# Scores of two query tiles in one three-bank PSUM tile, and two banks for projections, in the attention of a two-layer first block

## The chip, the cores and the metric

The kernel runs on one core of one Trainium2 chip. The metric is the device time of one execution in microseconds. One core has five engines that work side by side, each through its own queue in order: TensorE (PE, matmuls; its weight loads are shown apart as PEld), VectorE (DVE), ScalarE (ACT), GpSimd (POOL) and SyncE (SP, which issues most of the DMAs). Matmul results land in PSUM, which is 8 banks of 512 fp32 columns on 128 partitions; all eight are allotted in this kernel.

## The reference, cut to what matters

Two blocks follow each other on 512 tokens of width 1024: a first block of two layers, and a second block with one attention layer and a mixture of 32 experts. The change touches the first block alone. Each of its layers does this (x is 512 tokens, xc a context of 256 tokens; the second layer needs no output for the context):

```
h  = rms_norm(x)  * (1 + scale)   + shift        # scale, shift, gate: silu(c) @ w_mod + b_mod
hc = rms_norm(xc) * (1 + scale_c) + shift_c
parts = split(h @ w_in)                          # q and kv latents, gates, two convolution branches
k, v  = context and x tokens concatenated        # 256 + 512 = 768 keys, 8 heads of 96 (values of 64)

s = einsum('bqhd,bkhd->bhqk', q, k) * 96 ** -0.5
p = softmax(s, axis=-1)
attn = einsum('bhqk,bkhd->bqhd', p, v)

y = concat([attn * silu(g_a), short_conv_branch, long_conv_branch])
x = x + gate * (y @ w_out)                       # layer 0 does the same for xc, with the 256 context keys
```

## The kernel before

**Precision.** Every large product is made of three matmuls (`mm3`, lines 220 to 222): operands are split into a high and a low part (`split`: ACT writes the high part on line 183, DVE the low part on line 184), and high*high, high*low and low*high are added up in PSUM.

**A layer** (`layer`) first makes queries, keys and values and stores them in DRAM, while the projections `cf_a`, `cf_g` and `g_a` run beside that. Then comes the stretch that the change touches, the attention. It is a loop over 8 heads and, within a head, over groups of two query tiles of 128 tokens: three groups in layer 0 (two on the 512 x tokens with 768 keys, and g == 2 on the 256 context tokens with 256 keys), two groups in layer 1. That makes 24 steps in layer 0 and 16 in layer 1.

**One step.** `mla_scores` makes the scores `pS` of both query tiles (6 matmuls each for 768 keys: a piece of 512 columns and one of 256), DVE takes the negated row maximum (line 917) and scales it (918), ACT takes the exponential from PSUM into `P` with its row sum (920), DVE inverts the sum (921) and POOL scales `P` (922). `mla_out` then transposes `P` on PE, four 128x128 blocks to a bank (`pPT`, line 935), splits each bank into `PTh` (ACT) and `PTl` (DVE), and multiplies by the values (`pO`, line 945). The loop issues the scores of step s + 1 ahead of the transposes of step s. Between these pieces it lets other work in (`late`, a `Fill`, which hands out pieces by their cost): the remaining ten column projections (`cm`, bank `pcm`) and matmuls on the modulation weights (`mod_part`, bank `pmod`, read by ACT into `mrow` on line 329). At the end of the loop `norm_conv` (`pmean`, `pvar`, `prs`, `ppw`) finishes the long convolution branch. After the layer come `mod_gate` (`pgate`, line 355) and the output projection `out_proj` (`pout`).

**Order.** Nobody writes the order of these instructions down. The program gives them in the order of the code, and a scheduler with a cost model sorts them for each engine; the engines then run their queues strictly in order. A tile from a pool waits until the readers of the tile that had its place are done, and an instruction that writes a part of a tile waits for earlier readers of that tile.

**PSUM before.** Tag A: two tiles of two banks (`pa`: each query tile's scores has one, of which 768 of 1024 columns are used; also `pmean`, `prs`, `pkv`, `pq`, `pout`). Tag T: two banks (`pt`: transposes). Tag C: one bank (`pc`: `pcm`, `pmod`, `ppw`). Tag O: one bank (`po`: `pO`).

Of the kernel before, what the change touches and what calls it, by code (L numbers as in the profile page):

```python
# [10 lines left out]
F32 = mybir.dt.float32  # L11
# [20 lines left out]
PS2 = (3, 2, 2)  # L32
# [28 lines left out]
class Fill:  # L61
# [3 lines left out]
    def __init__(self, gens):  # L65
        self.gens, self.ready, self.debt = list(gens), [], 0.0
# [45 lines left out]
class K:  # L112
    def __init__(self, tc, I, out):
        self.tc, self.nc, self.I, self.out = tc, tc.nc, I, out
        self.es = ExitStack()
        self.nlo = 0
        self.single = False

    def pool(self, name, side=None, space=None, reuse="tile"):
        kw = {}  # L120
# [8 lines left out]
    def setup(self):  # L129
# [11 lines left out]
        self.ones = cp.tile([128, 128], F32, name="ones")  # L141
        nc.vector.memset(self.ones, 1.0 / 256)

    def pa(self, name="pa"):
        return self.ps.tile([128, 1024], F32, name=name, tag="A", bufs=2)

    def second_banks(self):
# [15 lines left out]
        return self.ps.tile([128, 512], F32, name=name, tag="T", bufs=PS2[1] if self.single else 2)  # L163

    def pc(self, name="pc"):
        return self.ps.tile([128, 512], F32, name=name, tag="C", bufs=PS2[2] if self.single else 1)

    def po(self, name="po"):
        return self.ps.tile([128, 512], F32, name=name, tag="O", bufs=1)
# [299 lines left out]
    def layer(self, l, hT, wl):  # L469
# [25 lines left out]
        for nm in ("q_head_norm_w", "k_head_norm_w"):  # L495
            w = self.brow(tr, I[nm][l][64:96], 32, "w32" + nm[0])
            t = tr.tile([128, 4, 2, 32], F32, name="tab" + nm[0])
# [11 lines left out]
        segs = [(0, 512)] if last else [(0, 512), (512, 256)]  # L509
# [183 lines left out]


        ap = self.pool(f"attn{l}", side="right")
        if not last:
            self.tables(ap)
        projs = [f(i) for i in range(2) for f in (sc_in, sc_c, sc_b, g_b)]
# [75 lines left out]

        for _ in tail:
            pass
        ap.release()
        lp.release()
        gp.release()
# [122 lines left out]
    def mla_scores(self, qkv, g, ap):  # L902

        nc, sp = self.nc, self.sp
        Q, Kt = qkv["q"], qkv["k"]
        segs = ((512, 768),) if g == 2 else ((0, 512), (512, 768))
        Ps = []
        for t in (2 * g, 2 * g + 1):
            pS = self.pa("pS")
            k0 = segs[0][0]  # L910
            for c0, c1 in segs:
                self.mm3(pS[:, c0 - k0:c1 - k0], [x[:, t * 128:(t + 1) * 128] for x in Q], [x[:, c0:c1] for x in Kt],
                         True, True)
            S = pS[:, :768 - k0]
            P = ap.tile([128, 768], F32, name="P", tag="P", bufs=PB)[:, :768 - k0]
            nm = sp.tile([128, 1], F32, name="nm", bufs=4)
            nc.vector.tensor_reduce(nm, S, axis=AX.X, op=OP.max, negate=True)  # L917
            nc.vector.tensor_scalar(nm, nm, SM1, None, op0=OP.mult)  # L918
            l = sp.tile([128, 1], F32, name="ll", bufs=4)
            nc.scalar.activation(P, S, AF.Exp, bias=nm, scale=SM1, accum_out=l)  # L920
            nc.vector.reciprocal(l, l)  # L921
            nc.gpsimd.tensor_scalar(P, P, l, 0.5, op0=OP.mult, op1=OP.mult)  # L922
            Ps.append(P)
        return Ps
# [1249 lines left out]
```

## Time and profile before

| | us |
|---|---|
| median of 3 runs | 1450.34 (1446.74 to 1450.8) |
| the profiled execution, whole | 1445.97 |
| its span, from the first to the last instruction | 1444.2 |
| attention of layer 0, first scores to last (start of the first matmul to the start of the last) | 181.5 to 416.3 |
| attention of layer 1, the same | 620.1 to 759.9 |

The profiled execution lies 4.4 us under the median and within the range of the runs; 1.8 us of it lie outside the span. A row of the timeline gives the start, the duration, the engine, the line of the kernel, the operation, what it writes and reads, how many were merged, and in square brackets how long the engine had been idle and what released it. Matmuls are pipelined: the time from one start to the next is what a matmul takes of PE, and the duration in the row is longer.

### The profile page before, as it was taken

What the parts mean: (1) busy time and instruction counts of PE and PEld (TensorE: products, weight loads), DVE (VectorE), ACT (ScalarE), POOL (GpSimd) and SP (SyncE); (2) the same over time, 40 slices, a digit from 0 to 9 for tenths busy, and PEclk for the clock granted to TensorE, in tenths of its full rate; (3) what the DMA queues carried; (4) which work ended last, traced back from release to release, by engine and by line L of the source; (5) the groups of instructions that cost most, each with busy time, mean ns of one, the idle gap of its engine ahead of it and who ended that gap; (6) DMA issues with size and microseconds to landing.
All of it is one profiled execution on the core that took longest, in us unless ns stands there. A gap on an engine that the chain in (4) does not pass through costs nothing. (4 is left out here: it accounts for less than half of the span.)

```text
span 1444.2 us, 22627 instructions
## 1 busy us (share of the span) xinstructions
PE 1313.0 (91%) x8030; PEld 1039.8 (72%) x8030; DVE 963.3 (67%) x2272; ACT 614.8 (43%) x1198; POOL 311.3 (22%) x397
## 2 busy tenths in 40 slices
PE   4999999998979999899999999999997999999873
PEld 2888777876867788677877788887777877675441
DVE  4689997565652589998775645777677553454555
ACT  4554255544641375256574335776654111112112
POOL 2332032222230134123322111111111111111101
PEclk9999999998999999999999999999998999999987
DMA  8643345435231255416144365323545689999971
GB/s 291 201 128 114 99 133 158 122 102 147 77 140 42 93 127 153 147 45 163 39 131 149 124 200 133 81 81 124 183 157 195 224 292 373 375 368 389 390 279 59
DMA packets 166917, 246.46 MB, mean 171 GB/s; under 512 B 46774, under 2 KB 102918, under 8 KB 166804
## 3 DMA queue, kind: packets, MB, share of 16 engines
q1 hardware_dynamic: 161460, 235.07, 49.3%
q0 software_dynamic: 4768, 7.84, 1.9%
q10 hardware_dynamic: 576, 2.10, 0.4%
q8 instruction: 64, 1.05, 0.3%
q14 instruction: 49, 0.40, 0.1%
HBM read 221.74 MB, written 33.33 MB: 177 GB/s over the span
## 5 line engine op out<-in xcount | busy, mean ns | idle before, releaser
L184 DVE TENSOR_TENSOR wlo<-wraw,whi 128x1024 fp32r<-128x1024 f32 (+3 forms) x98 | 119.0, 1220 | 60.6 <-ACT whi L183 60.1
L183 ACT ACTIVATE whi<-wraw 128x1024 fp32r<-128x1024 f32 (+3 forms) x98 | 100.6, 1036 | 106.2 <-PE pout L222 42.6
L922 POOL TENSOR_SCALAR P<-P,ll 128x768 f32<-128x768 f32 (+1 forms) x80 | 76.3, 958 | 187.0 <-DVE ll L921 103.3
L220 PE MATMUL pcm<-hTh,whi 128*128 128x256 f32 (+1 forms) x288 | 103.6, 360 | 9.9 <-DVE oa L529 4.3
L569 DVE SCALAR_TENSOR_TENSOR za<-zp,vec,za 128x783 f32<-128x783 f32 (+1 forms) x120 | 109.1, 916 | 0.5
L222 PE MATMUL pcm<-hTh,wlo 128*128 128x256 f32 (+1 forms) x288 | 100.1, 347 | 0.2 <-DVE wlo L184 0.2
L221 PE MATMUL pcm<-hTl,whi 128*128 128x256 f32 (+1 forms) x288 | 99.4, 345 | 0.0
L184 DVE TENSOR_TENSOR PTl<-pPT,PTh 128x512 fp32r<-128x512 f32 x104 | 70.3, 683 | 24.0 <-ACT PTh L183 23.7
L183 ACT ACTIVATE PTh<-pPT 128x512 fp32r<-128x512 f32 x104 | 60.2, 595 | 53.9 <-PE pPT L935 48.3
L920 ACT ACTIVATE P<-pS,nm 128x768 f32<-128x768 f32 (+1 forms) x80 | 64.9, 814 | 35.9 <-DVE nm L918 30.9
L1815 POOL DMA_INDIRECT xg<-h2d,tok x32 | 31.6, 987 | 207.8 <-PE pturn L1799 119.2
L917 DVE TENSOR_REDUCE nm<-pS 128x1 f32<-128x768 f32 (+1 forms) x80 | 66.4, 844 | 14.9 <-PE pS L222 14.2
L1421 POOL TENSOR_SCALAR P<-P,l 128x384 f32<-128x384 f32 (+1 forms) x64 | 34.2, 547 | 182.2 <-DVE m L1417 116.7
L220 PEld LDWEIGHTS pcm<-hTh,whi 128*128 128x128 f32 x288 | 55.5, 193 | 17.4 <-DVE oa L529 4.9
L220 PE MATMUL pcm<-hT0h,whi 128*128 128x512 f32 x144 | 59.3, 412 | 7.9 <-DVE oa L529 5.8
L935 PE MATMUL pPT<-ident,P 128*128 128x128 f32 x416 | 63.5, 279 | 3.3 <-POOL P L922 2.5
L1832 PE MATMUL pgu<-exT,eraw 128*128 128x128 f32 x512 | 60.9, 279 | 0.0
L222 PEld LDWEIGHTS pcm<-hTh,wlo 128*128 128x128 f32 x288 | 55.6, 193 | 6.8 <-DVE wlo L184 0.6
L1832 PEld LDWEIGHTS pgu<-exT,eraw 128*128 128x128 f32 x512 | 59.3, 194 | 1.3 <-DVE exT L1810 0.6
L221 PEld LDWEIGHTS pcm<-hTl,whi 128*128 128x128 f32 x288 | 55.5, 193 | 4.9 <-issue 0.2
L222 PE MATMUL pcm<-hT0h,wlo 128*128 128x512 f32 x144 | 58.0, 403 | 0.0
L221 PE MATMUL pcm<-hT0l,whi 128*128 128x512 f32 x144 | 57.9, 402 | 0.0
(535 smaller groups left out, 3670.7 us busy)
## 6 DMA issues: line engine op xcount, KB each, us to landing
wraw<-in_w_in_dram SPq DMA_DIRECT2D x56, 512.0 KB
eraw<-in_w_expert_gate_dram SPq DMA_DIRECT2D x52, 512.0 KB
eraw<-in_w_expert_up_dram SPq DMA_DIRECT2D x52, 512.0 KB
wraw<-in_w_mod_dram SPq DMA_DIRECT2D x48, 512.0 KB
wl<-in_w_expert_down_dram SPq DMA_DIRECT2D x32, 512.0 KB
wh<-in_w_expert_down_dram SPq DMA_DIRECT2D x32, 512.0 KB
wraw<-in_w_out_dram SPq DMA_DIRECT2D x24, 512.0 KB
wraw<-in_w_expert_gate_dram SPq DMA_DIRECT2D x12, 512.0 KB
```

What stands on the lines that cost most here:

```text
L183: nc.scalar.activation(hi, src, AF.Copy)
L184: return (eng or nc.vector).tensor_tensor(lo, src, hi.bitcast(F32), op=OP.subtract)
L220: mm(out, lhs[0], rhs[0], start=start, stop=False)
L221: mm(out, lhs[0], rhs[1], start=False, stop=False)
L222: mm(out, lhs[1], rhs[0], start=False, stop=stop)
L569: nc.vector.scalar_tensor_tensor(a[:, :nz], z[:, k:k + nz], cfw[:, i, k:k + 1], a[:, :nz], op0=OP.mult, op1=OP.add)
L917: nc.vector.tensor_reduce(nm, S, axis=AX.X, op=OP.max, negate=True)
L920: nc.scalar.activation(P, S, AF.Exp, bias=nm, scale=SM1, accum_out=l)
L922: nc.gpsimd.tensor_scalar(P, P, l, 0.5, op0=OP.mult, op1=OP.mult)
L935: nc.tensor.transpose(p[:, jj, i * 128:(i + 1) * 128], Ps[i][:, (j + jj) * 128:(j + jj + 1) * 128], self.ident)
L1421: nc.gpsimd.tensor_scalar(Ps[i], Ps[i], l[:, i:i + 1], 1.0, op0=OP.mult, op1=OP.mult)
L1832: self.last = self.nc.tensor.matmul(p[:, s, c, :], gu[2 * s + k // 4][:, k % 4, c * 128:(c + 1) * 128], x[:, k, :], start=(k == 0), stop=( ...
```

## The change

During the attention of both layers (from the point at which the projections ahead of it are done, to the end of `layer`) the PSUM pool is released and a pool with another division takes its place; at the end it is swapped back. In the new pool the scores have one tile of three banks (tag S, one buffer), the tag C has two banks, T two and O one. `mla_scores` now takes one tile for a step and puts the second query tile's scores behind the first's, at column 768, which is the middle of the second bank. Its pieces are cut at the bank's border: 256 and 512 columns in place of 512 and 256. The users of `pa` other than the scores (`pf` in `tables`, `pmean`, `prs`) take the tile S too while the attention runs.

```diff
+    def attention_banks(self, on):
+
+        self.ps.release()
+        self.ps = self.pool("psuma" if on else "psum", space=bass.MemoryType.PSUM)
+        self.attn = on
+
     def pa(self, name="pa"):
+        if self.attn:
+            return self.ps.tile([128, 1536], F32, name=name, tag="S", bufs=1)
         return self.ps.tile([128, 1024], F32, name=name, tag="A", bufs=2)
...
     def pc(self, name="pc"):
-        return self.ps.tile([128, 512], F32, name=name, tag="C", bufs=PS2[2] if self.single else 1)
+        return self.ps.tile([128, 512], F32, name=name, tag="C", bufs=2 if self.attn else PS2[2] if self.single else 1)
...
         ap = self.pool(f"attn{l}", side="right")
+        self.attention_banks(True)
...
         for _ in tail:
             pass
+        self.attention_banks(False)
         ap.release()
...
-        segs = ((512, 768),) if g == 2 else ((0, 512), (512, 768))
+        k0 = 512 if g == 2 else 0
         Ps = []
-        for t in (2 * g, 2 * g + 1):
-            pS = self.pa("pS")
-            k0 = segs[0][0]
-            for c0, c1 in segs:
+        pS2 = self.pa("pS")
+        for i, t in enumerate((2 * g, 2 * g + 1)):
+
+            pS = pS2[:, i * 768:i * 768 + 768]
+            for c0, c1 in ((512, 768),) if g == 2 else ((0, 256), (256, 768)) if i else ((0, 512), (512, 768)):
                 self.mm3(pS[:, c0 - k0:c1 - k0], [x[:, t * 128:(t + 1) * 128] for x in Q], [x[:, c0:c1] for x in Kt],
                          True, True)
```

The diff does not show what the scheduler makes of it. The number of matmuls, of reads of PSUM and of DMAs stays the same; their order moves on every engine. In the rows below a row is an instruction with its line, its output and inputs (the number behind a name is that of one tile), its size, and the semaphores on which it waits (`Activation` is ACT, `Pool` is POOL); "x4" is four alike.

PE, the last wide score pair of layer 0's head 7, before. Two tiles (4258 and 4273), their 12 matmuls back to back; the second tile waits only for the tile that had its place:

```order
L221 MATMUL pS_4258<-klo_3908,qhi_3911 128x512
L222 MATMUL pS_4258<-khi_3907,qlo_3912 128x512
L220 MATMUL pS_4258<-khi_3907,qhi_3911 128x256
L221 MATMUL pS_4258<-klo_3908,qhi_3911 128x256
L222 MATMUL pS_4258<-khi_3907,qlo_3912 128x256
L220 MATMUL pS_4273<-khi_3907,qhi_3911 128x512 [waits PE_49,Activation_49]
L221 MATMUL pS_4273<-klo_3908,qhi_3911 128x512
L222 MATMUL pS_4273<-khi_3907,qlo_3912 128x512
```

The same place now; both halves are the one tile 4240, and P_4170 and P_4184 are the two halves of the step before:

```order
L229 MATMUL pS_4240<-klo_3893,qhi_3896 128x512
L230 MATMUL pS_4240<-khi_3892,qlo_3897 128x512
L228 MATMUL pS_4240<-khi_3892,qhi_3896 128x256
L229 MATMUL pS_4240<-klo_3893,qhi_3896 128x256
L230 MATMUL pS_4240<-khi_3892,qlo_3897 128x256
L946 MATMUL pPT_4270<-ident_69,P_4184 128x128 [waits Pool_49]
L946 MATMUL pPT_4270<-ident_69,P_4170 128x128
L946 MATMUL pPT_4270<-ident_69,P_4184 128x128
L946 MATMUL pPT_4279<-ident_69,P_4184 128x128
L946 MATMUL pPT_4279<-ident_69,P_4170 128x128
L946 MATMUL pPT_4279<-ident_69,P_4184 128x128
L228 MATMUL pS_4240<-khi_3892,qhi_3896 128x256 [waits Activation_49]
```

The second half no longer follows the first: six transposes stand between them, and its first matmul waits for ACT.

PE, early in layer 0, where a modulation bank has been filled and read out (`mrow`) and a projection follows, before. There is one C bank, and `pcm_2293` needs it:

```order
L945 MATMUL pO_2166<-PTl_2212,vhl_1802 128x256 [waits DVE_49]
L945 MATMUL pO_2166<-PTl_2212,vhl_1802 128x256
L892 MATMUL pkT_2263<-ident_69,kraw_2123 96x128 [waits PE_49]
L892 MATMUL pkT_2263<-ident_69,kraw_2123 96x128
L222 MATMUL pS_2314<-khi_1794,qlo_1799 128x256
L220 MATMUL pcm_2293<-hTh_85,whi_2269 128x512 [waits PE_49,Activation_49]
L221 MATMUL pcm_2293<-hTl_86,whi_2269 128x512
L222 MATMUL pcm_2293<-hTh_85,wlo_2270 128x512 [waits DVE_49]
```

The first projection behind such a modulation bank now:

```order
L228 MATMUL pcm_2589<-hTh_85,whi_2552 128x512 [waits DVE_49,Activation_49]
L229 MATMUL pcm_2589<-hTl_86,whi_2552 128x512
L956 MATMUL pO_2165<-PTh_2171,vhl_1805 128x256 [waits DVE_49,Activation_49]
L956 MATMUL pO_2165<-PTh_2171,vhl_1805 128x256
L228 MATMUL pcm_2684<-hTh_85,whi_2552 128x256 [waits PE_49]
L229 MATMUL pcm_2684<-hTl_86,whi_2552 128x256
L230 MATMUL pcm_2589<-hTh_85,wlo_2553 128x512 [waits DVE_49]
L228 MATMUL pcm_2589<-hTh_85,whi_2552 128x512
```

Two projection tiles, 2589 and 2684, are open at once, in the two C banks.

PE at the end of layer 0's attention, before (`pout` is the output projection, `ppw` the last product of the long convolution branch):

```order
L222 MATMUL pS_4389<-khi_3907,qlo_3912 128x256
L220 MATMUL pout_4565<-whi_4490,hTh_85 128x512 [waits Activation_49]
L221 MATMUL pout_4565<-wlo_4491,hTh_85 128x512
L222 MATMUL pout_4565<-whi_4490,hTl_86 128x512
L220 MATMUL pout_4565<-whi_4490,hTh_85 128x512
L673 MATMUL ppw_4445<-lnd_4172,wraw_4357 128x512 [waits DMAHW1_49,DVE_49]
L935 MATMUL pPT_4461<-ident_69,P_4381 128x128 [waits Pool_49]
L221 MATMUL pout_4565<-wlo_4491,hTh_85 128x512
L222 MATMUL pout_4565<-whi_4490,hTl_86 128x512
L673 MATMUL ppw_4445<-lnd_4176,wraw_4357 128x512 [waits DVE_49]
```

And now, up to the first matmul of the output projection:

```order
L681 MATMUL ppw_4462<-lnd_4155,wraw_4338 128x256 [waits Activation_49]
L681 MATMUL ppw_4462<-lnd_4159,wraw_4338 128x256
L956 MATMUL pO_4440<-PTh_4446,vhl_3900 128x256 [waits DVE_49,Activation_49]
L956 MATMUL pO_4440<-PTh_4446,vhl_3900 128x256
L956 MATMUL pO_4440<-PTl_4447,vhl_3900 128x256 [waits DVE_49]
L956 MATMUL pO_4440<-PTl_4447,vhl_3900 128x256
L363 MATMUL pgate_4513<-ident_69,mod0_105 128x128 x4
L363 MATMUL pgate_4519<-ident_69,mod0_105 128x128 x4
L363 MATMUL pgate_4525<-ident_69,mod0_105 128x128 [waits Activation_49]
L363 MATMUL pgate_4525<-ident_69,mod0_105 128x128 x3
L363 MATMUL pgate_4531<-ident_69,mod0_105 128x128 [waits Activation_49]
L363 MATMUL pgate_4531<-ident_69,mod0_105 128x128 x3
```

The output projection moved from among `ppw` and the last transposes to behind the last `pgate`; in layer 1 it moved likewise.

## Rows read from the trace of the kernel before

**Rows 1.** The page's first section: busy time, share and count of each engine.

```profile
span 1444.2 us, 22627 instructions
PE 1313.0 (91%) x8030; PEld 1039.8 (72%) x8030; DVE 963.3 (67%) x2272; ACT 614.8 (43%) x1198; POOL 311.3 (22%) x397
```

**Rows 2.** Stretches: length, busy us of PE, PEld, DVE, ACT, POOL; granted clock; DMA.

```profile
181.00:428.00 247.00, 227.08 (x1478) 185.99 (x1476) 166.72 (x352) 124.03 (x253) 67.37 (x78) 0.95 0.42 127
621.00:774.00 153.00, 148.51 (x932) 121.30 (x931) 127.84 (x249) 95.39 (x181) 50.53 (x52) 0.99 0.35 97
210.00:225.00 15.00, 12.66 (x87) 9.22 (x88) 10.51 (x26) 7.94 (x18) 5.89 (x9) 0.89 0.68 209
760.00:770.00 10.00, 8.81 (x55) 7.33 (x54) 9.19 (x23) 5.40 (x11) 3.74 (x5) 0.83 0.39 138
```

**Rows 3.** PE's waits from 175 to 428 us: total us, times, longest.

```profile
PE pS L220 <- ACT P L920: 3.7, 4, 2.0
PE pO L945 <- ACT PTh L183: 2.4, 5, 0.7
PE pPT L935 <- POOL P L922: 2.3, 2, 1.2
...
PE pcm L220 <- ACT mrow L329: 1.8, 1, 1.8
PE pO L945 <- DVE nm L918: 1.5, 2, 1.2
...
PE pcm L220 <- ACT u L593: 0.8, 1, 0.8
```

**Rows 4.** PE's waits from 610 to 785 us.

```profile
PE pcm L220 <- DVE u L603: 0.9, 1, 0.9
PE pcm L220 <- ACT u L593: 0.7, 1, 0.7
```

**Rows 5.** Timeline, layer 0: one tile's scores, maximum and exponential, undisturbed.

```profile
233.49 0.28 PE L222 MATMUL pS<-khi,qlo 96*128 96x256 f32 x1
233.61 0.39 PE L220 MATMUL pS<-khi,qhi 96*128 96x512 f32 x1
233.81 0.96 DVE L917 TENSOR_REDUCE nm<-pS 128x1 f32<-128x768 f32 x1 [0.56 <-PE pS L222]
...
235.07 0.90 ACT L920 ACTIVATE P<-pS,nm 128x768 f32<-128x768 f32 x1 [3.17 <-DVE nm L918]
...
235.87 0.19 ACT L920 ACTIVATION_READ_ACCUMULATOR P<-pS,nm 128x1 f32 x1
```

**Rows 6.** Timeline, layer 1: the same with another DVE instruction ahead of the scaling.

```profile
621.79 0.52 PE L222 MATMUL pS<-khi,qlo 96*128 96x256 f32 x2
622.11 1.82 DVE L917 TENSOR_REDUCE nm<-pS 128x1 f32<-128x768 f32 x2
...
623.85 0.14 DVE L918 TENSOR_SCALAR nm<-nm 128x1 f32<-128x1 f32 x1
624.09 0.90 ACT L920 ACTIVATE P<-pS,nm 128x768 f32<-128x768 f32 x1
...
624.88 0.19 ACT L920 ACTIVATION_READ_ACCUMULATOR P<-pS,nm 128x1 f32 x1
```

**Rows 7.** Timeline: matmuls of 512 and 256 columns and transposes in unbroken runs.

```profile
233.84 0.40 PE L221 MATMUL pS<-klo,qhi 96*128 96x512 f32 x1
234.07 0.40 PE L222 MATMUL pS<-khi,qlo 96*128 96x512 f32 x1
...
235.45 0.28 PE L220 MATMUL pcm<-hTh,whi 128*128 128x256 f32 x1
235.57 0.28 PE L221 MATMUL pcm<-hTl,whi 128*128 128x256 f32 x1
```

**Rows 8.** Timeline, layer 0: eight transposes and what PE starts next.

```profile
401.68 1.04 PE L935 MATMUL pPT<-ident,P 128*128 128x128 f32 x8
402.47 0.37 PE L220 MATMUL pcm<-hTh,whi 128*128 128x256 f32 x1
```

**Rows 9.** Timeline: the first output projection of each layer, and a late pgate.

```profile
417.69 0.50 PE L220 MATMUL pout<-whi,hTh 128*128 128x512 f32 x1 [1.09 <-ACT P L920]
...
434.71 1.05 PE L355 MATMUL pgate<-ident,mod 128*128 128x128 f32 x7 [1.01 <-ACT gate L357]
...
772.52 0.39 PE L220 MATMUL pout<-whi,hT0h 128*128 128x512 f32 x1
...
782.43 0.82 PE L355 MATMUL pgate<-ident,mod 128*128 128x128 f32 x5
```

More of the change, by code (lines that the diff above doesn't have):

```diff
@@ L116, in __init__ @@
         self.nlo = 0
-        self.single = False
+        self.single = self.attn = False
     def pool(self, name, side=None, space=None, reuse="tile"):
```

## The prediction

> **What bounds the kernel now.** The page's first section names the engine that could be the bound: PE is busy for 91% of the span, and no other engine comes near it [rows 1]. Such a share is a mean over unlike stages, so the stretch that changes is read next. In the attention of layer 0 PE is busy for 227.1 of 247 us, in that of layer 1 for 148.5 of 153, at a granted clock of 0.95 and 0.99; DVE, the next, has 168 and 128 us [rows 2]. There PE itself is the bound: what makes PE stand still lengthens the program, and at most 19.9 and 4.5 us can be won by taking idle time away. What follows (convolution, output projection, the second block) waits for the attention's output, so I count a delay one to one. Then come the waits of PE in these stretches. In layer 0 they are small and many: 3.7 us for the exponential that frees a scores tile, 2.4 for `PTh`, 2.3 for the scaled `P`, 1.5 for a row maximum (by `nm` into `pO`), and two waits of projections for the only C bank, 1.8 and 0.8 us [rows 3]. In layer 1 the C bank costs 0.9 and 0.7 us [rows 4], and no wait for a scores tile is among the listed ones.
>
> **Second C bank.** The four C waits go: 1.8 + 0.8 + 0.9 + 0.7 = 4.2 us. The 1.8 us wait lies in a stretch of 15 us with a clock of 0.89 [rows 2]; if this idle time brought the clock down, 15 x (1 - 0.89) = 1.65 us, an estimate, come back as well. The order shows that the bank is used: two `pcm` tiles open at once where one had to wait. What is late next there is the weights' low part (`wlo`, DVE), a wait that stood there before too.
>
> **Scores in one tile.** The matmuls are the same in number and size, and cutting at 256 and 512 rather than 512 and 256 costs nothing. What changes is the wait. Before, both halves of a step ran back to back into two tiles, and each tile waited for the exponential of the tile one whole step back, for which PE had mostly no wait. Now the order has the second half waiting for ACT's exponential of the first half of the same tile, and the first half of the next step waiting for that of the second. Two tiles deep has become one half deep. Layer 0 has 48 halves and layer 1 has 32, so 47 + 31 = 78 such waits are added; 32 + 31 = 63 of them stand behind a wide half (768 keys) and 15 behind a narrow one.
>
> What does one wait for? The last score matmul starts at 233.49, the maximum runs from 233.81 for 0.96 us, the exponential starts at 235.07, and its accumulator read ends at 235.87 + 0.19 = 236.06: a chain of 236.06 - 233.61 = **2.45 us**, counted from the moment at which PE could go on, with DVE and ACT undisturbed [rows 5]. With one other DVE instruction ahead of the scaling it is 624.88 + 0.19 - 621.91 = **3.2 us** (the second of the merged matmuls starts 0.12 after 621.79) [rows 6]. In the changed order DVE stands between maximum and scaling with nothing in 18 of 80 cases, and with something else (mostly a `PTl`, an `ot` or a `wlo`) in the rest, so the truth lies between; I take 2.8, nearer the middle than either row.
>
> What PE does meanwhile is whatever its queue holds between the halves, since the queue is in order: behind a waiting score stand transposes, `pO` products and projections that could run and don't. A 512-column matmul takes 234.07 - 233.84 = 0.23 us of PE and one of 256 takes 0.12 [rows 7]; a transpose takes (402.47 - 401.68) / 8 = 0.10 [rows 8]. So the six transposes between the halves of tile 4240 are 0.6 us against 2.45: 1.8 us of idle PE, where there was none. Counting every gap in the changed order in this way (with 0.118 for a transpose, 0.12 for `pO`), 19 of the 63 wide gaps hold less than 2.45 us of work, 26 less than 2.8 and 40 less than 3.2. The missing time adds up to
>
> - chain of 2.45 us: 8.2 in layer 0 + 6.8 in layer 1 = 15.0 us;
> - 2.8 us: 12.6 + 10.4 + 0.5 for the narrow ones (put at 1.9) = 23.5 us;
> - 3.2 us: 20.3 + 16.4 + 1.2 (narrow at 2.2) = 37.9 us.
>
> Against this the old waits for scores tiles, 3.7 us [rows 3], are gone, being replaced. Of the chain waits `pO` for `PTh`, `pPT` for `P` and `pO` for `nm`, 2.4 + 2.3 + 1.5 = 6.2 us [rows 3], I take half (3.1; bounds 0 and 6.2): a PE that stands still at a score gives these operands time.
>
> [...] PE's waits for C show a matmul group held until ACT or DVE has read the bank [rows 3, 4]. [...]
>
> **Ends of the attentions.** Before, 14 `pout` matmuls of layer 0 began at 417.69, ahead of the last `pgate` at 434.71, and 20 of layer 1 at 772.52, ahead of 782.43 [rows 9]. They filled a tail that is a chain of small steps. Now `pout` stands behind the last `pgate` in both layers: up to 34 x 0.235 = 8.0 us (bounds 0 and 8). I take 6, since `ppw` and transposes are left to fill a part. The tail stretch 760 to 770 was granted 0.83 although PE was busy for 8.81 of 10 us [rows 2], which costs 10 x 0.17 = 1.7 us. With stalls I expect one more such stretch in each layer: +3.4 us, an estimate (bounds 0 and 7).
>
> **Other things that move.** `pf`, `pmean` and `prs` share the scores tile; they are few, and `ppw` and transposes stand beside them (0 to 2 us, taken as nothing). POOL's scaling of `P` follows ACT, its queue holds little else (67 of 247 us busy [rows 2]), and it pushes nothing. SP's loads of `w_mod` are issued earlier in layer 0, ahead of weights that `pcm` needs; DMA engines are busy for 0.42 there [rows 2], so I take nothing, and 3 us either way, as for the order of the second block, which moves in places too.
>
> **The sum**, on the profiled execution: +23.5 - 3.7 - 3.1 - 4.2 - 1.6 + 6 + 3.4 = +20.3, and 1445.97 + 20.3 = 1466. The median of the runs lies 4.4 us above the profiled execution, so about **1470** for the median. With every term at its lower end the sum is 15.0 - 3.7 - 6.2 - 4.2 - 1.6 = -0.7, with every term at its upper one 37.9 - 9.5 + 8 + 7 = +43; not all fall on one side, so I give the likeliest case 1455 to 1490.
>
> **The rivals.**
> (a) *The cover suffices: faster.* The scheduler placed these gaps. In layer 1 before, waits of the same kind cost PE nothing that its list of waits shows [rows 4], and PE's real passage through a gap is longer than its counted matmuls, since other waits (weights, `PTh`, `P`) lie in the same gaps. If each gap lasts half a microsecond longer than counted and the chain stays at 2.45, the wide ones miss 4.5 + 3.4 = 7.9 us in place of 15. Then +7.9 - 3.7 - 4.2 - 1.6 - 6.2 with a filled tail gives -7.8, some 1442 for the median (1434 to 1446). It decides as soon as the visible chain is about 2 us or less. Against it: 26 gaps are shorter than a chain with any company on DVE, some are as short as 0.24 and 0.7 us, and the C bank is worth only 4.2 us.
> (b) *It cancels.* Chain at 2.45, no loss in the tail, no more clock lost: +15.0 - 3.7 - 4.2 - 1.6 - 3.1 = +2.4, 1446 to 1455.
> (c) *The score chain becomes the bound of layer 1.* One half takes PE 3 x 0.23 + 3 x 0.12 = 1.05 us, and its chain 3.2; 32 of these in a row are 136 us, and the stretch from the first scores to the last was 139.8. Should DVE or ACT add half a microsecond to each chain, layer 1 alone grows by some 12 us, beyond the stalls at 3.2: +37.9 + 12 + 8 + 3.4 - 3.7 - 4.2 - 1.6 = +52, about 1502, and over 1490 already with a part of it. For it: DVE is busy for 128 of 153 us [rows 2], so that a maximum will often find it occupied. Against it: the gaps with much work are already longer than the chain.
> (d) *It does not do what it says* (the second bank unused, the halves not in series): the order shows both, which leaves no chance worth a number.
>
> **How the numbers follow.** About 0.3% (4 us) is what a measurement of this kernel can tell from no change. Forecast 0.60, (a) 0.18, (b) 0.13, (c) 0.09. Faster by over 0.3% is (a), 0.18; within is (b), 0.13; slower is the forecast and (c), 0.69. The range leaves half of (a) out below and (c) out above, which is nearly 2 in 10: 1443 to 1490. The likeliest case's own range is 1455 to 1490.
>
> **What would show it.** In the profile after: waits of PE at the score lines for ACT's exponential, near 24 us in total in some 25 to 40 pieces of 0.3 to 2.5 us, in both layers; no wait of `pcm` for `mrow` or `u` left; PE's busy time unchanged but for the clock; the attention of layer 0 at some 255 us and that of layer 1 at 165; `pout` starting behind the last `pgate`, with idle PE between. I am wrong if these score waits sum to under 10 us, or if they are there and time comes back elsewhere (shorter waits at `PTh`, `P` and `nm`, a higher clock, earlier weights), or if the second block moves by more than the 3 us that I left it.

## The result and the profile after

The changed kernel takes 1470.26 us (median of 4 runs, 1467.67 to 1472.31), the kernel before in the same comparison 1448.54. The ratio is 1.0155, with a 95% interval of 1.013 to 1.018: slower by some 22 us, clear of noise, and 1470 us had been forecast (+20.3 us by its sum). The total is right. Where the time was lost is not where the forecast put it, and that is what the rest is about.

The first lines of the profile after, against [rows 1]: the same work, a longer span.

```profile
span 1466.6 us, 22620 instructions
PE 1329.4 (91%) x8030; PEld 1045.9 (71%) x8030; DVE 972.0 (66%) x2272; ACT 615.9 (42%) x1198; POOL 306.7 (21%) x397
```

To find the place I cut both executions at the same events, read from the timelines (starts of the first and last score matmul of a layer, of the last `pout`, of the first matmul of the second block's attention, and the end of the last DMA issue). The last three columns are experiments that are told of below: "layer 0 alone" has the change there only, "layer 1 alone" likewise, "swap alone" has the new pool with the old division. Each column is one execution; that of "layer 0 alone" is the longest of its twelve (1449.3 us, median 1442.35).

| us | before | after | layer 0 alone | layer 1 alone | swap alone |
|---|---|---|---|---|---|
| up to layer 0's first scores | 181.5 | 180.5 | 181.9 | 178.4 | 182.3 |
| layer 0, first scores to last | 234.8 | 230.4 | 230.8 | 231.2 | 233.4 |
| from there to its last `pout` | 88.3 | 88.2 | 87.8 | 88.3 | 91.8 |
| from there to layer 1's first scores | 115.4 | 113.9 | 115.7 | 113.3 | 115.2 |
| layer 1, first scores to last | **139.8** | **165.0** | 140.4 | **165.2** | 139.8 |
| from there to its last `pout` | 64.9 | 67.7 | 66.3 | 69.1 | 72.5 |
| to the second block's attention | 53.0 | 54.2 | 54.5 | 54.5 | 53.0 |
| from there to the end | 556.7 | 557.0 | 559.9 | 557.9 | 556.4 |

Layer 1's scores have lost 25.2 us, and its tail 2.8. Layer 0 has lost nothing: its scores are 4.4 us shorter in this pair of profiles. With "layer 1 alone" layer 0's PE has the order of the kernel before, and still took 231.2 rather than 234.8 us, so a good part of the 4.4 us is what one execution differs from another by.

The next fence gives the stretches of after that stand against [rows 2] (columns as there), the second line for layer 1's attention, and then layer 1 in pieces.

```profile
181.00:428.00 247.00, 230.05 (x1490) 183.97 (x1489) 170.02 (x355) 128.64 (x259) 67.35 (x79) 0.96 0.42 129
621.00:774.00 153.00, 138.51 (x811) 107.42 (x810) 116.44 (x213) 87.75 (x165) 44.01 (x45) 0.96 0.33 93
613.00:728.00 115.00, 111.45 (x669) 86.32 (x668) 94.38 (x168) 65.61 (x123) 33.79 (x35) 1.00 0.40 109
728.00:753.00 25.00, 18.44 (x92) 14.42 (x90) 17.09 (x32) 12.92 (x25) 6.62 (x8) 0.83 0.33 94
753.00:778.00 25.00, 20.25 (x111) 15.99 (x111) 15.63 (x31) 13.47 (x26) 5.73 (x7) 0.90 0.00 0
778.00:800.00 22.00, 16.66 (x81) 12.78 (x80) 12.64 (x28) 7.47 (x13) 5.10 (x7) 0.77 0.09 33
```

And layer 1 of the kernel before, in pieces of the same kind:

```profile
620.00:740.00 120.00, 116.70 (x740) 95.04 (x740) 98.33 (x189) 71.25 (x137) 40.60 (x42) 1.00 0.37 98
740.00:760.00 20.00, 20.00 (x118) 16.33 (x116) 18.64 (x35) 16.97 (x31) 5.88 (x6) 1.00 0.29 90
760.00:780.00 20.00, 18.56 (x103) 14.20 (x102) 15.10 (x35) 9.22 (x17) 5.39 (x8) 0.91 0.26 95
```

Up to 728 us PE is as full as before (97% against 97%) at a granted clock of 1.00. Then come 50 us of scores in which it is busy for 38.69 us only, at a granted clock of 0.83 and 0.90. The last projection says why the border lies at 728, and three row maxima give the pace (the first of layer 1, the 21st of 32, and the last):

```profile
614.91 0.95 DVE L928 TENSOR_REDUCE nm<-pS 128x1 f32<-128x768 f32 x1
...
720.62 0.95 DVE L928 TENSOR_REDUCE nm<-pS 128x1 f32<-128x768 f32 x1
...
727.84 0.39 PE L230 MATMUL pcm<-hT0h,wlo 128*128 128x512 f32 x1
...
778.37 0.96 DVE L928 TENSOR_REDUCE nm<-pS 128x1 f32<-128x768 f32 x1
```

And from the kernel before, its last projection and its last row maximum (the first of its layer 1 starts at 622.11 [rows 6]):

```profile
756.55 0.39 PE L222 MATMUL pcm<-hT0h,wlo 128*128 128x512 f32 x1
...
761.24 0.94 DVE L917 TENSOR_REDUCE nm<-pS 128x1 f32<-128x768 f32 x1
```

The halves follow each other every (720.62 - 614.91) / 20 = 5.29 us while there are projections, and every (778.37 - 720.62) / 11 = 5.25 us when there are none. Before, the interval was (761.24 - 622.11) / 31 = 4.49 us, and PE had work for nearly all of it. So the halves in series run at a pace of their own, some 0.8 us longer. While projections last, the surplus is filled with them, and they are used up early: the last projection starts at 727.84, behind 22 of the 32 halves and 50 us ahead of the last scores. Before, it stood behind 30 halves, 3 us ahead of the last scores, and PE was still full in the last 20 us (740 to 760). After that the surplus is idle time.

Taken apart over the 31 intervals of layer 1 in the timeline after, an interval is on the mean 1.16 us from the first score matmul of a half to the start of its last, 3.54 us from there to the end of the exponential's accumulator read, and 0.60 us until the next half starts. In 21 of the 31 the next half starts within 0.25 us of that end: mostly it is the exponential that the next half waits for.

One half of that stretch, in the timeline after:

```profile
768.72 0.40 PE L230 MATMUL pS<-khi,qlo 96*128 96x512 f32 x1
...
769.15 0.96 DVE L928 TENSOR_REDUCE nm<-pS 128x1 f32<-128x768 f32 x1 [0.20 <-PE pS L230]
...
770.04 0.42 DVE L977 TENSOR_TENSOR ot<-pO,ot 64x256 f32<-64x256 f32 x1
770.38 0.14 DVE L929 TENSOR_SCALAR nm<-nm 128x1 f32<-128x1 f32 x1
...
770.61 0.90 ACT L931 ACTIVATE P<-pS,nm 128x768 f32<-128x768 f32 x1 [0.60 <-DVE nm L929]
771.41 0.19 ACT L931 ACTIVATION_READ_ACCUMULATOR P<-pS,nm 128x1 f32 x1
...
771.65 0.61 PE L228 MATMUL pS<-khi,qhi 96*128 96x512 f32 x1 [1.85 <-ACT P L931]
...
772.06 0.63 PE L229 MATMUL pS<-klo,qhi 96*128 96x512 f32 x1
...
772.49 0.63 PE L230 MATMUL pS<-khi,qlo 96*128 96x512 f32 x1
```

The last score matmul starts at 768.72, the maximum and, behind an `ot` on DVE, its scaling follow, then the exponential, and the next half starts at 771.65: 2.9 us, of which PE stands still for 1.85. That is the chain that the prediction took from [rows 5, 6]; by its count (from 0.23 us behind the start of the last matmul) it is 2.65 us here. This half has one of the shortest chains, though: by that count the mean is 3.4 us, in layer 1 and behind the wide halves of layer 0 alike, above the longer of the two rows (3.2). What the prediction did not take either is in the last rows: these matmuls of 512 columns start 0.42 us apart and not 0.23 [rows 7], so that behind this wait one took PE 1.8 times as long. The granted clock was 1.00 from 769 to 771.6 and 0.61 from there to 776.

### The profile page after: what moved, and what is told of

It is laid out like the page before. It is cut to its first block, busy times and chain, and to the rows that moved or that the text cites. A ratio compares the mean times of both kernels' runs of the same rounds, so it can differ in the third digit from the quotient of the medians.

```text
span 1466.6 us, 22620 instructions
## 1 busy us (share of the span) xinstructions
PE 1329.4 (91%) x8030; PEld 1045.9 (71%) x8030; DVE 972.0 (66%) x2272; ACT 615.9 (42%) x1198; POOL 306.7 (21%) x397
## 5 line engine op out<-in xcount | busy, mean ns | idle before, releaser
L933 POOL TENSOR_SCALAR P<-P,ll 128x768 f32<-128x768 f32 (+1 forms) x80 | 70.5, 882 | 256.1 <-DVE ll L932 222.1
L228 PE MATMUL pcm<-hTh,whi 128*128 128x256 f32 (+1 forms) x288 | 100.1, 348 | 4.9 <-ACT whi L191 2.5
L928 DVE TENSOR_REDUCE nm<-pS 128x1 f32<-128x768 f32 (+1 forms) x80 | 67.7, 846 | 29.2 <-PE pS L230 28.4
L946 PE MATMUL pPT<-ident,P 128*128 128x128 f32 x416 | 71.0, 293 | 11.1 <-POOL P L933 8.4
L946 PEld LDWEIGHTS pPT<-ident,P 128*128 128x128 f32 x416 | 51.4, 149 | 24.1 <-POOL P L933 17.3
L228 PE MATMUL pS<-khi,qhi 96*128 96x256 f32 (+1 forms) x144 | 54.9, 381 | 10.7 <-ACT P L931 8.2
```

Of the source, the lines that this page charges most:

```text
L228: mm(out, lhs[0], rhs[0], start=start, stop=False)
L946: nc.tensor.transpose(p[:, jj, i * 128:(i + 1) * 128], Ps[i][:, (j + jj) * 128:(j + jj + 1) * 128], self.ident)
```

## The experiments

Theory A, formed on this comparison: waiting for the other half's exponential costs where there are no projections left to cover it, in layer 1. Rivals: B, layer 1's loss comes from layer 0's changed order; C, it is the swap of the pools and the output projection behind it; D, each half in series costs a fixed time whatever stands between. Times are medians, ratios against the kernel before on the same chip.

**Layer 0 alone** (label e1). Both swaps stand under a condition, and scores in the old pool take a tile each:

```diff
-        self.attention_banks(True)
+        if l == 0:
+            self.attention_banks(True)
```

> The changed allotment in layer 0 alone; layer 1 has the old tiles (PE's order in layer 1 is that of the kernel before). Theory A (waiting for one half's exponential costs only where the projections that fill the gaps have run out, which happens in layer 1): layer 0 keeps its gain of 7 us up to the first scores of layer 1 and nothing is lost behind it, so 1441 to 1443 against 1448.5, faster than both. Rival B (layer 1's loss of 28 us is inherited from the changed order of layer 0, through loads or projections that come at other times): 1455 or more. Rival C (the swap of the pools and the output projection behind it cost, in each layer alike): half of the tails' loss is kept, 1445 to 1449.

1442.35 us against 1445.18, ratio 0.9978 (0.9959 to 0.9996). As theory A has it, layer 1 is back at 140.4 us, and B is out. Layer 0's gain is real but about 3 us, less than half of the 7 that A expected, and the time alone would also fit C (0 to 3.5 us faster than 1448.5). Against C speaks layer 0's tail, which stands before a swap and is not longer (87.8 us).

**Layer 1 alone** (e2, `if l == 1`).

> The changed allotment in layer 1 alone. Theory A: the whole loss of layer 1, 28 us from its first scores to the last output projection, so 1475 to 1478, slower than the changed kernel itself by the 7 us that layer 0 gave. Rival B: 1450 to 1460. Rival C: half of the loss, about 1460.

1472.2 us, ratio 1.018 (1.0155 to 1.0206): 26 us slower, close to A's 26.5 to 29.5 over 1448.5, with layer 1 at 165.2 us. The whole loss belongs to layer 1; the changed kernel's 1.0155 is this and layer 0's 3 us.

**Swap alone** (e3). The pools are swapped, with the old division (one bank for projections, pieces of 512 and 256 columns) and a tile for each query tile:

```diff
-        if self.attn:
-            return self.ps.tile([128, 1536], F32, name=name, tag="S", bufs=1)
...
-        pS2 = self.pa("pS")
...
+            pS = self.pa("pS")
```

> The pools are swapped as in the change, but the new one has the old division (scores in two tiles of two banks, one bank for projections). Theory A: nothing but the tails, where the output projection waits for the release: 0 to +5 us, 1448 to 1453. Rival C: +10 us or more, 1458 and up, with idle PE ahead of the output projections.

1457.25 us, ratio 1.0075 (1.0055 to 1.0095): 11 us. This is rival C's number, and theory A's guess for the tails was too low. The table says where: the tails are 3.5 us longer in layer 0 and 7.6 in layer 1, and the scores are unchanged (139.8 us in layer 1). PE in layer 1's tail, after the swap alone:

```profile
783.35 3.78 PE L679 MATMUL ppw<-lnd,wraw 128*128 128x512 f32 x4 [0.84 <-ACT za L680]
786.93 2.22 PE L361 MATMUL pgate<-ident,mod 128*128 128x128 f32 x16
788.90 0.48 PE L226 MATMUL pout<-whi,hT0h 128*128 128x512 f32 x1
```

The first `pout` stands behind the last `pgate`, as in the changed kernel. So the swap has a price; it is not what the changed kernel lost, though, as its own tails are 0.1 us shorter and 2.8 us longer. A part of the reason is in the traces: behind the last scores of layer 1 stand 24 transposes and 24 `pO` products in the kernel before and after the swap alone, but 12 and 17 in the changed kernel, which had done the others ahead of them. That this is the whole reason is not shown.

**One bank for projections** (e4). The scores share a tile as in the change, the tag C keeps one bank, and one bank is unused:

```diff
-... tag="C", bufs=2 if self.attn else PS2[2] if self.single else 1)
+... tag="C", bufs=PS2[2] if self.single else 1)
```

> The scores in one tile of three banks in both layers, but one bank for projections (one bank is unused). Theory A: in layer 1 the projections are paced by their one bank and reach to the 28th of the 32 halves rather than the 22nd, so the stretch from the first scores to the last is 148 to 155 us rather than 165; in layer 0 the gain of the second bank (4 to 6 us) is missing, first scores to last pgate 246 to 250 rather than 242.6: together 1458 to 1466. Rival (the halves in series cost the same 2 us or so in each gap, whatever the projections do): layer 1 as in the changed kernel, 165 us, and the time 1474 to 1478 for want of the bank's gain.

1475.43 us, ratio 1.0211 (1.0173 to 1.025). Neither expectation holds. Layer 1's scores take 158.0 us, 7 less than with two banks (theory A had said 148 to 155, its rival 165): the projections come more slowly through one bank and reach further (the last starts behind 28 halves, as A had it, not 22), and the last 26 us of the scores have PE fuller (21.59 of 26 us) and at a granted clock of 1.00,

```profile
760.00:786.00 26.00, 21.59 (x124) 16.34 (x123) 21.16 (x39) 17.47 (x33) 7.34 (x8) 1.00 0.30 97
```

but layer 0's scores take 246.2 us, 15.8 more than in the changed kernel, where 4 to 6 had been expected. With the scores in series the second bank is thus worth 16 us in layer 0, and it costs 7 in layer 1. What halves in series cost by themselves is 246.2 - 233.4 = 13 us in layer 0 and 158.0 - 139.8 = 18 in layer 1, both against the swap alone. Each kernel has the order that the scheduler made for it, so these are prices of an allotment together with its order.

**More work to fill with** (e5, e6). Four more column projections (`more`: `cm` with a copy into a tile that nobody reads) go into layer 1's `late` list, in the kernel before and in the changed one; the estimate of work by which `Fill` hands out the pieces is raised with them (14 projections for 10):

```diff
-        late += [g_c(0), g_c(1)]
+        late += [g_c(0), g_c(1)] + [more(i) for i in range(4 if last else 0)]
```

> The kernel before with four more column projections in layer 1's attention (4 x 24 matmuls of 512 columns, their results are not used; the output stays what it was). PE is full there, so they cost 96 x 0.235 = 22.6 us: 1466 to 1472, by every theory.

> The changed kernel with the same four projections. Theory A (the loss sits in the last 50 us of layer 1's scores, where no projections are left to cover one half's exponential): the additional 22.6 us of matmuls go into idle time, and cost only 2 to 10 us over the changed kernel: 1472 to 1480, so that the loss against the same addition to the kernel before shrinks from 22 to 4 to 10 us. Rival D (each half in series costs a fixed time, whatever stands between): they cost the whole 22.6 us, 1491 to 1495, and the loss stays at 22 us.

The kernel before takes 1474.98 us with them, ratio 1.0206 (1.0185 to 1.0228), and its scores in layer 1 go from 139.8 to 167.3, more than the 22.6 us of their matmuls that had been forecast. The changed one takes 1483.89, ratio 1.0261 (1.0236 to 1.0285), and goes from 165.0 to 182.1. The same addition costs 27.5 us where PE is full and 17.1 where it was idle, so the loss in this stretch falls from 25.2 to 14.8 us in the profiled executions. That of e6 (1490.26) is the longest of its four; by the medians the loss against the same addition is 1483.89 - 1474.98 = 8.9 us, which is within A's 4 to 10. That speaks against D, by which it stays at 22. Over the changed kernel A had expected less (2 to 10 us; by the ratios it is 15): the added projections end before the scores too, the last behind 28 halves, and in the profiled execution the last 17 us of the scores (780 to 797) have PE at a granted clock of 0.51.

```profile
780.00:797.00 17.00, 12.68 (x43) 10.24 (x44) 5.71 (x12) 5.31 (x10) 2.73 (x3) 0.51 0.07 26
```

**A short chain** (e7, e8). The row maximum and its scaling are left out, so that the chain is the exponential alone:

```diff
-            nc.vector.tensor_reduce(nm, S, axis=AX.X, op=OP.max, negate=True)
-            nc.vector.tensor_scalar(nm, nm, SM1, None, op0=OP.mult)
...
-            nc.scalar.activation(P, S, AF.Exp, bias=nm, scale=SM1, accum_out=l)
+            nc.scalar.activation(P, S, AF.Exp, bias=0.0, scale=SM1 * 1e-3, accum_out=l)
```

> The kernel before without the row maximum and its scaling (the exponential takes no offset and a thousandth of the scale, so that it stays finite; the softmax is another one). It takes 80 maxima and scalings off DVE, of which PE rarely waits: 1438 to 1447.

> The changed kernel without the row maximum and its scaling, in the same way. The chain from a half's last matmul to the end of its exponential falls from 2.45 to 3.2 us to about 1.2. Theory A: PE hardly waits for it any more, layer 1 from the first scores to the last is 140 to 147 us, and the kernel is within 6 us of the same cut in the kernel before. Rival D (the loss is in the series and the order of the matmuls themselves, not in the length of the chain): 15 us or more above it.

1465.36 and 1464.13 us: some 20 us above the kernel before, which had not been expected of either; against each other they are within the 6 us that A allowed, where D had 15 or more. The stretches explain the 20 us: from the second block's attention to the end both take some 594 us, not 557, with 8126 matmuls on the page instead of 8030. The other softmax gives the second block other tokens to distribute among its experts (argued, not tried), so only the first block can be compared. There the last `pout` starts at 805.6 us in the kernel before and at 802.4 in the changed one. Layer 1's scores take 142.4 and **140.5** us. With a short chain the halves in series cost nothing, and PE is full to the end of the changed kernel's scores:

```profile
594.00:736.00 142.00, 140.24 (x865) 111.65 (x865) 92.98 (x167) 89.51 (x174) 44.27 (x49) 1.00 0.37 103
```

This is the clearest verdict for A over D: series, tile and swap are all there, and the loss is gone with the chain. It does not part the two halves of A, since the scheduler's order moved as well: the last projection now starts behind 30 of the 32 halves, not 22. The same projections spread as far at the old length of the chain were not tried; e4 comes nearest, where they reach to 28 halves and 18 us are lost all the same. A second thing was not looked for: layer 0's scores, with the old tiles, fall from 233 (the mean of 234.8, 231.2 and 233.2 in the three executions with this order) to 216.6. They too had been waiting for the chain, or for DVE, which loses 0.96 us a maximum here; e9 below shortens the chain alone and takes them to 224.8.

**The scaling folded away** (e9 to e11). The factor goes once into the columns that scale the queries, so that the chain loses its shortest link, and the softmax is what it was:

```diff
+        nc.vector.tensor_scalar(qk[:, 0:2], qk[:, 0:2], SM1, None, op0=OP.mult)
...
-            nc.vector.tensor_scalar(nm, nm, SM1, None, op0=OP.mult)
...
-            nc.scalar.activation(P, S, AF.Exp, bias=nm, scale=SM1, accum_out=l)
+            nc.scalar.activation(P, S, AF.Exp, bias=nm, scale=1.0, accum_out=l)
```

> The kernel before with the factor 96^-0.5 multiplied once into the columns by which the queries are scaled (qk, one DVE instruction a layer), so that the 80 scalings of the row maximum fall away and the exponential takes the maximum as it is: the chain of a half is 0.3 us shorter. In the kernels without a maximum (chain 1.2 us shorter) layer 0's scores took 18 us less: if that goes with the length of the chain, 4 us are gained, 1438 to 1443 against 1444.5; if it came from DVE's load of 0.96 us maxima, 0 to 1 us.

> The changed allotment in layer 0 alone, with the folded scaling in both layers. If the gains add up: 3 us for layer 0's allotment and 0 to 4 for the shorter chain, a little more of it where halves are in series: 1436 to 1442, faster than both kernels. If the two gains are one and the same idle time: as the better of the two alone.

> The changed kernel with the folded scaling. Theory A: the 11 halves of layer 1 behind the last projection are paced by the chain and gain 0.3 us each, 3 us, the shorter gaps ahead of them as much again: 4 to 8 us faster than the changed kernel, 1459 to 1463. Rival D: as much as the kernel before gains by it.

| | us | ratio to before | layer 0's scores | layer 1's scores |
|---|---|---|---|---|
| before, folded (e9) | 1439.8 | 0.9962 (0.9947 to 0.9977) | 224.8 | 141.4 |
| layer 0 alone, folded (e10) | 1442.79 | 0.9983 (0.9972 to 0.9994) | 226.4 | 141.4 |
| changed, folded (e11) | 1453.69 | 1.0067 (1.005 to 1.0083) | 227.8 | 154.8 |

The changed kernel gains 0.9% by it, some 13 us: more than twice what the kernel before gains, and more than A's 4 to 8 us. Its first and last row maximum of layer 1 give the pace:

```profile
610.64 0.95 DVE L929 TENSOR_REDUCE nm<-pS 128x1 f32<-128x768 f32 x1
...
764.18 0.95 DVE L929 TENSOR_REDUCE nm<-pS 128x1 f32<-128x768 f32 x1
```

(764.18 - 610.64) / 31 = 4.95 us, against (778.37 - 614.91) / 31 = 5.27: 0.32 us less in the mean interval, about the length of the link taken out (0.3 us, from the end of the maximum to the start of the exponential in [rows 5]). That the two agree is in part chance. The time between maximum and exponential fell by 0.51 us on the mean (0.99 to 0.48), because other DVE instructions had stood before the scaling as well, and the next half then starts 0.28 us later behind its chain (0.88 against 0.60). The projections reach to the 26th half instead of the 22nd. A had expected the gain of the 11 halves without projections; it holds on the mean of all 31. So theory A needs its second half: the chain sets the pace of the whole layer, and its price shows up where the projections have run out. The gains of layer 0's allotment and of the fold do not add up (e10 is no faster than e9), as if they took the same idle time. The kernel before with the fold is the fastest of all, ahead of both kernels.

## Why the prediction came out, point by point

**What bounds the kernel.** Right for layer 1: PE was full there, and what was lost came through one to one (28.0 us in layer 1, less 7.1 gained ahead of it and with 1.5 lost behind it, are the 22.4 us by which the span grew). For layer 0 it was too simple: e7 and e9 take 16 and 8 us from its scores by a shorter chain, in a stretch that was read as bound by PE. The 227 of 247 us busy [rows 2] include the pipelined ends of matmuls (0.40 us long at starts 0.23 apart [rows 7]).

**The waits.** The mechanism was right, the place was not. The prediction put 12.6 us in layer 0 and 10.4 in layer 1. Waits of PE and its weight loads at scores for ACT's exponential, in the whole first block, after, and then before (us, times; weight loads run beside matmuls, after for 1045.9 us beside 1329.4 in a span of 1466.6, so this is not all time in which PE stands still):

```profile
  ACT P L931: 25.0, 32
```

```profile
  ACT P L920: 10.2, 12
```

On PE itself, without the weight loads, they are 3.6 us in 3 pieces in layer 0, much as before (3.7 in 4 [rows 3]), and 4.6 in 4 in layer 1, together 8.2. By its own mark (under 10 us in the list of PE's waits) the prediction counts as wrong on this step. The remainder of layer 1's loss shows as other things: waits for `P` and `klo`, and a granted clock of 0.83 and 0.90. These are PE's waits from 728 to 778 us (total, times, longest):

```profile
PE pS L228 <- ACT P L931: 4.6, 4, 2.1
PE pqT L902 <- DVE klo L907: 2.2, 2, 1.3
PE pPT L946 <- POOL P L933: 1.2, 1, 1.2
```

The step that failed is the static count of work between the halves. It weighed each gap alone. It did not ask where the projections would be used up, which costs layer 1 more than twice what was counted, nor that in layer 0 the gaps hold more time than their matmuls. Its chain of 2.8 us was too short as well: measured are 3.4 behind wide halves and 2.4 behind narrow ones (put at 1.9). By its own list a chain of 3.2 alone is 20.3 us in layer 0, where PE waited 3.6 us for the exponential, so the count of the gaps erred the other way. The kernel before could have told: there the same chain was 3.9 us on the mean of all wide halves, and the two halves of [rows 5, 6] are short ones.

One term that was taken as nothing shows once: `pmean` takes the scores' tile in layer 1 from 760.61 us, and DVE's reading of it holds the next scores until 764.01, 3.5 us behind the end of the exponential:

```profile
760.61 1.93 PE L645 MATMUL pmean<-za,ones 128*128 128x512 f32 x4
...
764.01 0.47 PE L228 MATMUL pS<-khi,qhi 96*128 96x512 f32 x1 [0.71 <-DVE lnd L652]
```

**The rivals.** (a), "the cover suffices", looks like what happened in layer 0, but only with the second bank: by e4 against the swap alone, halves in series cost 13 us there (12.6 + 0.5 were counted, before the waits that they replace are taken off), and the bank took them away again. (c), "the score chain becomes the bound of layer 1", is what happened in layer 1. Its working (16.4 us of stalls at a chain of 3.2, and some 12 beyond) is 28 us for layer 1; measured are 25.2 in the scores and 2.8 in the tail. The forecast's total was met by luck, because two errors cancel. By the sum's terms layer 0 was to lose 12.6 + 0.5 - 3.7 - 3.1 - 2.6 - 1.6 + 2.5 + 1.7 = 6.3 us and layer 1 10.4 - 1.6 + 3.5 + 1.7 = 14.0 (tails by their 14 and 20 `pout`, the clock by halves). Measured are -4.5 up to layer 0's last `pout` and +28.0 in layer 1.

**The second bank.** The waits of [rows 3, 4] for `mrow` and `u` are gone, as forecast. But 4.2 us was the worth of the bank to the old order. In the new one it is worth 16 us to layer 0 and costs layer 1 7 (e4 against the changed kernel). What it would be worth beside scores in two tiles was not tried: the eight banks that the kernel allots do not hold both (4 for the scores, 2 for T, 2 for C and 1 for O are nine). The scores' halves in series in one tile, in place of two tiles in turn, cost 13 us in layer 0 and 18 in layer 1 (e4 against the swap alone).

**The tails.** The order had `pout` behind the last `pgate`, and so it was (first `pout` at 426.57 and 799.56 us). The term of 6 us was too small for the swap alone (11 us measured, above its bound of 8.0), and in the changed kernel only 2.7 of it remained.

**The clock.** Mis-sized, by a factor of three. 3.4 us were expected; from 728 to 800 us the rows give 25 x 0.17 + 25 x 0.10 + 22 x 0.23 = 11.8 us, against 20 x 0.09 = 1.8 us in the same tail before, so 10 more (length x missing clock, the prediction's own measure). By this estimate it is a good third of layer 1's loss. Over the whole execution the granted clock went from 0.967 to 0.960, which by the same measure is 11 us.

**The second block** stayed within the 3 us left to it: 1.5 us from the last `pout` to the end.

## What to carry to other kernels

When a tile loses its second buffer, don't only add up what each gap lacks. Take the length of the chain from all its occurrences, not from two clean ones, and work out the pace that it allows (here 5.27 us a half), set it against the pace at which the engine was full (4.49 us), and ask whether the filling lasts to the end at that pace; the loss appeared here where it ran out, in 50 us at a granted clock of 0.83 and 0.90. And look at the short links: a scaling of 0.14 us on one column, with its hand-over, was worth 0.3 us on the mean of 31 intervals, and some 5.5 us in the kernel before, where PE had seemed to be the bound.

## What the runs showed of the hardware

Behind the wait of 1.85 us that ended at 771.65 matmuls of 512 columns started 0.42 us apart, against 0.23 us in unbroken runs, and the granted clock up to 776 was 0.61. In the three stretches from 728 to 800 us, in which PE was busy for 74 to 81%, the granted clock was 0.77 to 0.90; it was 0.51 in one of e6 with 75%, and 1.00 in one of e4 with 83%. What sets it is not shown. By length x missing clock, an estimate, the lower clock cost some 10 us in layer 1 beside 15.5 us of additional idle time (the gaps between matmuls in the timeline, from the first scores to the last `pout`, add up to 20.7 us against 5.3).

One and the same order of PE in layer 0's attention took 234.8, 231.2 and 233.2 us in three executions, which is as much as most terms of the prediction's sum for that layer.
